# Feed-forward block of an encoder layer: the second norm's sum of squares on POOL, the order of the last weight sum's products, and the buffers of the late halves' weights

## The chip, the cores and the metric

The kernel runs on one core of one Trainium2 chip. The metric is the device time of one execution in microseconds (us), the median of several runs. The core's engines are PE (TensorE, matmuls), DVE (VectorE), ACT (ScalarE), POOL (GpSimd) and SP (SyncE, which here only issues DMAs). Each works through its own list of instructions strictly in order and waits, where an operand or a buffer isn't ready, with everything behind it in the list waiting too.

## The reference

The kernel computes one layer of an encoder trunk on 1024 tokens of width 1024: two groups of mixing heads, an output projection, a squared-ReLU MLP with hidden width 4096, and a gated embedding. What matters here is the MLP, whose input is normalised:

```python
z = jnp.einsum('bsd,df->bsf', rms_norm(h, norm2_g[i]), w_ff1[i])
h = h + jnp.einsum('bsf,fd->bsd', jnp.square(jax.nn.relu(z)), w_ff2[i])
```

The norm divides each token by the root of its mean square, which is a positive factor. The kernel therefore multiplies the un-normalised h with the weights first and applies the factor (the tile `Rb`, one value per token, spread over all partitions) to the products afterwards.

## The kernel before

All matmuls take 32-bit numbers that are split into a rounded part (hi) and the rest (lo), and make three passes: hi with hi, hi with lo, lo with hi. ACT writes a hi part and DVE the lo part (`split`, L138 and L141). A matmul instruction multiplies 128 rows with 512 columns.

The first MLP matmul (FF1) runs in 16 chunks c of 256 hidden columns. Chunks 2 to 15 use a scheme with seven products of 512x512 blocks in place of eight: the blocks of h (tiles `b`, made once) meet four weight tiles per chunk that `sw_prep` makes from the raw weights: a (raw), then after four sums of weight blocks (L231 to L234) b, c and d, where d is the weight sum `s` that only the last product, named s1, reads. Every product is 4 k-steps of 3 passes, so a chunk is 7 x 12 = 84 matmuls. The sums over the products (L260, in chunk 2 L1284) are DVE's. The four weight sums are DVE's in chunks 2 and 3 and POOL's from chunk 4 on. Chunk 2 is `first_prods`, which takes three products one after the other and then interleaves the other four by k-step.

Beside chunk 2, `squares` (L1241 to L1247) sums the squares of h, eight tiles of 1024 tokens in two halves of 512: ACT squares one half tile into `sq`, and an add collects it into `Rb`; the first half's seven adds are POOL's, the second half's DVE's. `sq` has one buffer for each half, so the next square of a half waits for the add of the one before. The sums then go through PE (`n2ps`, L167), DVE (`n2ms`), POOL (`n2rs`, the root), PE again (`n2R`, L179, spreads it) and ACT into `Rb` (L180). From then on `finish(c)` applies it: ReLU times `Rb` on DVE (L1355), the square on ACT (L1356), and `z_blocks` makes block sums on POOL (L1370 to L1376) and stores all of it to four arrays in DRAM, one for each sweep of the second matmul. The stores stand in the queues of SP and ACT.

Chunks 0 and 1 are done without the scheme. Their halves over the first 512 tokens come early (`first_half`), the other halves after chunk 15 (`second_half`, matmuls `p0b` and `p1b`, 48 each), with weights `w1q` that `plain_w` loads and splits into the same ring of two hi and two lo buffers (pool `wp`) in which the chunks' weights and the second matmul's weights live.

The second MLP matmul (FF2, L1503 `f_P`) runs in four sweeps over the chunks, in the order 2, 0, 1, 3. Of sweep 2, `ff2_early` prepares the first three chunks: it loads z back (`zr`), splits it (`zh` on ACT, L1342, and `zl` on DVE) and splits the weights. The order of instructions on each engine comes from a scheduler that works from the program's order, its buffers and its own estimates.

Tiles made with `utile` take a buffer of a ring of 16; the blocks of h, the block sums `tz` and the z tiles live in it too.

Of the kernel before, what the change touches and what calls it, by code (L numbers as in the profile page):

```python
# [14 lines left out]
ALU = mybir.AluOpType  # L15
# [44 lines left out]
def tile_block(ctx, tc, xT, pT, w_in, w_out, w_ff1, w_ff2, w_gate, w_up, vecs, gate_b, rpbp, con,  # L60
# [3 lines left out]
    V, S, G, TE = nc.vector, nc.scalar, nc.gpsimd, nc.tensor  # L64

    def dump(name, ap):
        if name in dbg:
            nc.sync.dma_start(dbg[name], ap)
# [9 lines left out]
    def utile(name):  # L78
        return big.tile([P, T], F32R, tag="u", bufs=16, name=name)

    def utile32(name):
        return big.tile([P, T], F32, tag="u", bufs=16, name=name)
# [24 lines left out]
    Rb = cp.tile([P, T], F32, name="Rb")  # L107
# [27 lines left out]
    def split(pool, raw, n, tag, name, bufs=None, act_hi=True, lo_eng=None, hl=None):  # L135
        hi, lo = hl or [pool.tile([P, n], F32R, tag=tag + x_, name=name + x_, bufs=bufs) for x_ in "hl"]
        if act_hi:
            mark["hi"] = S.activation(hi, raw, AF.Copy).ins  # L138
        else:
            V.tensor_copy(hi, raw)  # L140
        mark["lo"] = (lo_eng or V).tensor_tensor(lo, raw, hi.bitcast(F32), op=ALU.subtract).ins  # L141
        return hi, lo
# [13 lines left out]
    def wview(w, k0, k1, c0, c1):  # L156
        return w[k0 * P : k1 * P, c0:c1].rearrange("(k p) n -> p k n", p=P)

    def passes(ahi, alo, bhi, blo):
        return ((ahi, bhi), (ahi, blo), (alo, bhi))  # L160
# [189 lines left out]
    with tc.tile_pool(name="m0", bufs=2) as m0:  # L350
# [57 lines left out]
        for e in range(8):  # L408
            up = htile(f"up{e}")
            es = slice(e * P, (e + 1) * P)  # L410
            for hf in range(2):
                hs = slice(hf * 512, (hf + 1) * 512)
# [301 lines left out]
    with tc.tile_pool(name="m1", bufs=2) as m1:  # L714
# [159 lines left out]
        def natten_first():  # L874

            kr, qr = raw_load(1, wp, "wr", 3), raw_load(0, wp, "wr", 3)
            yield
            kh, kl = htile("kh0", F32R), htile("kl0", F32R)
            for half in range(2):
                for _ in k_part(0, kr, kh, kl, half):  # L880
                    pass
            yield
            qs = [q_views(htile(f"q0_{rb}", F32R)) for rb in range(2)]
            for rb in range(2):
                for _ in q_part(0, qr, *qs[rb], rb):
                    pass
            nat[0] = [kh, kl, *qs]
            yield

        pre = natten_first()  # L890
# [31 lines left out]
    with tc.tile_pool(name="m2", bufs=2) as m2, tc.tile_pool(name="m2p", bufs=2, space=PSUM) as m2p:  # L922
# [169 lines left out]
        def prep(n):  # L1092

            pr, u = divmod(n, 8)
            if pr and u == 1:
                late.append(q_part(pr, qrs.pop(pr), *nat[pr][3], 1))
            if pr == 3:
                return
            if u in (3, 4):
                late.append(k_part(pr + 1, krs[pr + 1], nat[pr + 1][0], nat[pr + 1][1], u - 3))  # L1100
            if u == 5:
                late.append(q_part(pr + 1, qrs[pr + 1], *nat[pr + 1][2], 0))
# [15 lines left out]
        with tc.manual_schedule():  # L1118
# [9 lines left out]
            for n in range(NU):  # L1128
# [41 lines left out]
                if n in (1, 4, 6):  # L1170
                    j = {1: 0, 4: 1, 6: 2}[n]
# [20 lines left out]
    with tc.tile_pool(name="ff1", bufs=1) as ff1:  # L1192
# [46 lines left out]
        def squares():  # L1239

            sq = utile32("sq2")  # L1241
            for k in range(KT):
                for half in range(2):
                    hs = slice(half * 512, (half + 1) * 512)
                    S.activation((sq if k else Rb)[:, hs], hres[k][:, hs], AF.Square)
                    if k:
                        (V if half else G).tensor_tensor(Rb[:, hs], Rb[:, hs], sq[:, hs], op=ALU.add)  # L1247

        def plain_w(nm, f, hl=None):

            r = wp.tile([P, T], F32, tag="wr", name=f"{nm}_{f}r", bufs=3)
            nc.sync.dma_start(r.rearrange("p (k n) -> p k n", n=P), wview(w_ff1, 0, 8, f * P, (f + 1) * P))
            return [t_.rearrange("p (k n) -> p k n", n=P) for t_ in split(wp, r, T, "w", f"{nm}_{f}", hl=hl)]
# [14 lines left out]
        def first_prods(nm, w, z):  # L1268

            c11, c12, c21, u2 = z[0][:, 0:512], z[0][:, 512:], z[1][:, 0:512], z[1][:, 512:]  # L1270
            names = (("11", "11"), ("12", "21"), ("s4", "22"), ("s2", "t2"), ("s3", "t3"), ("22", "t4"), ("s1", "t1"))
            ps = {an: ps_(f"{nm}_{an}_{bn}") for an, bn in names}

            def part(an, bn, j):
                for i, (x_, y_) in enumerate(passes(w[an][0][:, j], w[an][1][:, j], *B[bn, j])):
                    TE.matmul(ps[an], x_, y_, start=j == 0 and i == 0, stop=j == 3 and i == 2)

            for an, bn in names[:3]:
                for j in range(4):
                    part(an, bn, j)  # L1280
            for j in range(4):
                for an, bn in names[3:]:
                    part(an, bn, j)
            add = lambda o, a, b: V.tensor_tensor(o, a, b, op=ALU.add)  # L1284
            S.activation(u2, ps["11"], AF.Copy)
            add(c11, u2, ps["12"])
            add(u2, u2, ps["s2"])
            add(c12, u2, ps["s4"])
            add(u2, u2, ps["s3"])
            add(c21, u2, ps["22"])  # L1290
            add(c12, c12, ps["s1"])
            add(u2, u2, ps["s1"])

        def prep(c, mid=None):
            s1 = ff1.tile([P, 512], F32, tag="s1", name=f"s1_{c}")
            return sw_prep(f"w1_{c}", [wview(w_ff1, 0, 8, (2 * c + f) * P, (2 * c + f + 1) * P) for f in range(2)],
                           s1, V if c < 4 else G, mid)

        def ff2_early(c):
            return zsplit(utile32(f"zr2_{c}"), utile(f"zh2_{c}"), utile(f"zl2_{c}"), zd[2][:, c]), w2_blocks(2, c)  # L1300
# [39 lines left out]
        def zsplit(raw, hi, lo, src):  # L1340
            nc.sync.dma_start(raw, src)
            S.activation(hi, raw, AF.Copy)  # L1342
            dv.append(V.tensor_tensor(lo, raw, hi.bitcast(F32), op=ALU.subtract).ins)  # L1343
            return hi, lo
# [37 lines left out]
        def relu2(z, hs):  # L1382
            V.scalar_tensor_tensor(z, z, 0.0, Rb[:, hs], op0=ALU.max, op1=ALU.mult)
            S.activation(z, z, AF.Square)
# [40 lines left out]
        for e in range(8):  # L1425
            dump(f"h1_{e}", hres[e])

        def second_half(c):

            zb, z0 = utile32(f"z{c}c"), utile32(f"z{c}d")  # L1430
            nc.sync.dma_start(z0, zd[2][:, c])
            for i, hs in enumerate((h0, h1_)):
                plain(f"p{c}b{i}", [wq.pop(0)], b12, bs("22"), ((4, 5, 6, 7), (0, 1, 2, 3)), (zb[:, hs],))
                if (c, i) != (1, 1) and len(wq) < 2 and wn:
                    wq.append(plain_w("w1q", wn.pop(0)))
                relu2(zb[:, hs], h1_)
            z_blocks(c, zb[:, h0], zb[:, h1_], z0[:, h1_], z0[:, h0])

        for c in range(3, NC_):
            products(c, w, 0)  # L1440
            if c == NC_ - 1:
                b12 = []
                for j in range(4):
                    t_ = ff1.tile([P, T], F32R, tag="b", bufs=NB, name=f"b12_{j}")
                    hi, lo = t_[:, h0], t_[:, h1_]
                    S.activation(hi, hres[j][:, h1_], AF.Copy, scale=vcol(V_G2, j))
                    V.scalar_tensor_tensor(lo, hres[j][:, h1_], vcol(V_G2, j), hi.bitcast(F32), op0=ALU.mult, op1=ALU.subtract)
                    b12.append((hi, lo))

            rs2 = []  # L1450
            sw_prods(f"p{c}", w, B, zt[c], 1, ps_, (lambda: rs2.append(sumsq_to_rstd(Rb, range(KT), "n2"))) if c == 3 else None)
            if c == 3:
                bcast_rstd(rs2[0], range(KT), "n2")
                finish(2)
            if c + 1 < NC_:
                w = prep(c + 1)
            else:
                wn = [2, 3]
                wq = [plain_w("w1q", f) for f in range(2)]
            finish(c)  # L1460
            if c in (5, 6):
                z0 = utile32(f"z{c - 5}b")
                nc.sync.dma_start(z0, zd[2][:, c - 5])
                for hs in (h0, h1_):
                    relu2(z0[:, hs], h0)
                nc.sync.dma_start(zd[2][:, c - 5], z0)
        pre = [ff2_early(0)]
        second_half(0)
        second_half(1)
        pre += [ff2_early(1), ff2_early(2)]  # L1470


    with tc.tile_pool(name="ff2", bufs=2) as ff2:
# [56 lines left out]
        half = lambda r, t, j: hres[4 * r + j][:, t * 512 : (t + 1) * 512]  # L1530
# [53 lines left out]
        op, _ = ff2_sweep(2, 0, ("P2", "P1"), pre, {}, 0)  # L1584
        op, _ = ff2_sweep(0, 1, ("P3", "P6"), op, {}, 2)
# [10 lines left out]
        op, _ = ff2_sweep(1, 3, ("P5", "P7"), op, {EC + ES * c: [(early, c)] for c in range(NE)}, 1)  # L1596
# [103 lines left out]
```

## Time and profile before

| | us |
|---|---|
| runs | 1416.90, 1417.74, 1419.88; median 1417.74 |
| profiled execution, its own time | 1419.03 |
| its span, first to last instruction | 1417.3 |
| PE busy | 1334.9 (94%) |
| DVE busy | 902.3 (64%) |
| ACT busy | 599.0 (42%) |
| POOL busy | 517.6 (37%) |

The span is the stretch that the trace covers; the 1.7 us between it and the execution's own time lie around it. The granted clock, a mean over the span, is 0.965 of full speed. A busy share is a mean over stages with different limits, so it says only which engine to look at first; where an engine stood still is read from the waits, and when, from the timeline.

### The profile page before, as it was taken

Reading aid. Unit: us, or ns where it says so; the run is one execution under the profiler, and the core shown is the slowest. Engines: PE = TensorE matmul, PEld = TensorE weight load, DVE = VectorE, ACT = ScalarE, POOL = GpSimd, SP = SyncE. Lnnn points to the kernel's source line nnn. Section 1 sums busy time; section 2 is a strip of 40 time slices with the busy share of each in tenths; the row PEclk is TensorE's granted clock in tenths of the full one; section 3 lists DMA queues with packets and bytes.
Section 4 is the critical chain, followed back from the end, with each engine's and each line's share of the span. In section 5 each row is a group of like instructions: output and inputs, shape, how many; then the busy total and the mean of one; then the engine's idle time right before and its main releaser. Section 6 shows DMA issues by size and latency. Waiting matters only on the chain. (4 is left out here: it accounts for less than half of the span.)

```text
span 1417.3 us, 19403 instructions
## 1 busy us (share of the span) xinstructions
PE 1334.9 (94%) x7139; PEld 1110.6 (78%) x7139; DVE 902.3 (64%) x1422; ACT 599.0 (42%) x985; POOL 517.6 (37%) x406
## 2 busy tenths in 40 slices
PE   7999999999999889999899999999699899999998
PEld 6988778799888567787777788887488678888887
DVE  4486886665762646578556766675247898559443
ACT  7353443364554535535333333343234234445321
POOL 2215675463421111100256665654102661007422
PEclk9999999999998899999999999999899899999999
DMA  8543333475323644213234555447866683452342
GB/s 282 199 148 93 107 108 105 173 225 160 109 68 124 186 141 133 93 60 105 60 104 156 178 164 163 153 143 239 292 202 205 202 263 105 151 161 73 101 146 82
DMA packets 158158, 211.27 MB, mean 149 GB/s; under 512 B 17904, under 2 KB 106992, under 8 KB 158064
## 3 DMA queue, kind: packets, MB, share of 16 engines
q1 hardware_dynamic: 149968, 192.07, 42.7%
q10 hardware_dynamic: 6624, 12.06, 2.5%
q0 software_dynamic: 1472, 5.92, 1.2%
q8 instruction: 56, 0.92, 0.3%
q14 instruction: 38, 0.31, 0.1%
HBM read 155.79 MB, written 54.21 MB: 148 GB/s over the span
## 5 line engine op out<-in xcount | busy, mean ns | idle before, releaser
L1343 DVE TENSOR_TENSOR zl<-zr,zh 128x1024 fp32r<-128x1024 f32 x56 | 79.8, 1432 | 15.5 <-ACT zh L1342 15.5
L966 POOL TENSOR_SCALAR pc<-pc,st 128x288 f32<-128x288 f32 (+1 forms) x32 | 17.6, 548 | 159.6 <-DVE st L961 128.0
L1324 POOL TENSOR_TENSOR w2re<-sk,w2re 128x512 f32<-128x512 f32 x16 | 32.0, 2002 | 113.6 <-DVE sk L1323 103.2
L1342 ACT ACTIVATE zh<-zr 128x1024 fp32r<-128x1024 f32 x56 | 58.3, 1047 | 17.1 <-DMA zr<-zd 17.1
L956 ACT ACTIVATE pc<-pc,st 128x288 f32<-128x288 f32 (+1 forms) x64 | 36.3, 569 | 57.9 <-DVE st L955 57.9
L1503 PE MATMUL f_P<-zl,w2h 128*128 128x512 f32 x128 | 52.9, 413 | 5.4 <-DVE zl L1343 5.3
L955 DVE CUSTOM_DVE_ANT_1 pc<-sc,tab 128x288 f32<-128x288 f32 (+1 forms) x64 | 29.9, 504 | 41.9 <-DMA tab<-tabU 23.7
L1503 PE MATMUL f_P<-zh,w2h 128*128 128x512 f32 x128 | 51.5, 402 | 1.2 <-ACT zh L1342 1.2
L1503 PE MATMUL f_P<-zh,w2l 128*128 128x512 f32 x128 | 51.7, 404 | 0.0
L1572 PE MATMUL g<-gh,wg_h 128*128 128x512 f32 (+1 forms) x136 | 51.7, 380 | 0.0
L1572 PE MATMUL g<-gl,wg_h 128*128 128x512 f32 (+1 forms) x136 | 51.2, 377 | 0.0
L1572 PE MATMUL g<-gh,wg_l 128*128 128x512 f32 (+1 forms) x136 | 51.1, 377 | 0.0
L1526 POOL TENSOR_TENSOR h<-h,evP 128x512 f32<-128x512 f32 x8 | 14.8, 1887 | 98.3 <-ACT evP L1517 98.3
L790 POOL TENSOR_SCALAR wv<-vh,wj 128x129 f32<-128x129 f32 x56 | 31.0, 556 | 54.1 <-PE num L791 49.6
L1370 POOL TENSOR_TENSOR tz<-z,z 128x512 f32<-128x512 f32 x14 | 18.6, 1330 | 72.3 <-ACT z L1356 72.3
L260 DVE TENSOR_TENSOR z<-z,p_s_t 128x512 f32<-128x512 f32 x52 | 34.5, 683 | 15.9 <-PE p_s_t L256 14.6
L138 ACT ACTIVATE w_bh<-w_0r 128x1024 fp32r<-128x1024 f32 x14 | 14.9, 1062 | 68.3 <-POOL w_0r L234 59.5
L1355 DVE SCALAR_TENSOR_TENSOR z<-z,Rb 128x1024 f32<-128x1024 f32 x28 | 41.3, 1486 | 3.6 <-ACT Rb L180 3.6
L1578 DVE TENSOR_TENSOR z<-g,Rb 128x512 f32<-128x512 f32 (+1 forms) x17 | 11.0, 659 | 43.4 <-PE g L1572 37.5
L997 PE MATMUL pv<-pT,vw 128*64 128x128 f32 (+1 forms) x384 | 31.9, 295 | 6.1 <-DVE pT L986 3.2
L1356 ACT ACTIVATE z<-z 128x1024 f32<-128x1024 f32 x28 | 29.5, 1057 | 19.2 <-DVE z L1355 19.1
L1329 ACT ACTIVATE w2h<-w2ro 128x512 fp32r<-128x512 f32 x16 | 10.1, 632 | 63.9 <-PE f_P L1503 21.1
(861 smaller groups left out, 4780.3 us busy)
## 6 DMA issues: line engine op xcount, KB each, us to landing
zr<-zd SPq DMA_DIRECT2D x56, 512.0 KB
w2r<-w_ff SPq DMA_DIRECT2D x48, 256.0 KB
zd<-z ACTq DMA_DIRECT2D x42, 256.0 KB
zd<-tz SPq DMA_DIRECT2D x32, 256.0 KB
w2re<-w_ff SPq DMA_DIRECT2D x16, 512.0 KB
w2ro<-w_ff SPq DMA_DIRECT2D x16, 512.0 KB
w_0r<-w_ff SPq DMA_DIRECT2D x14, 512.0 KB
w_1r<-w_ff SPq DMA_DIRECT2D x14, 512.0 KB
```

The source lines that it names most:

```text
L260: mark["add"] = V.tensor_tensor(o, a, b, op=ALU.add).ins
L790: G.tensor_scalar(wv, vh[:, c, 0:129], wj[:, col], 1.0, op0=ALU.mult, op1=ALU.mult)
L955: V.tensor_tensor_reduce(pb, sc.rearrange("p a b -> p (a b)"), tab[:, s], -1.0, -NEG, ALU.add, ALU.min, st[:, 0:1])
L956: S.activation(pb, pb, AF.Exp, scale=-1.0, bias=st[:, 0:1], accum_out=st[:, 1:2])
L997: TE.matmul(pv[e0 : e0 + 64, cb], vws[pr][: 4 * kw, cb, rb + j, e0 : e0 + 64], pT[s][: 4 * kw, j], start=j == 0, stop=j == 2)
L1324: G.tensor_tensor(a21, s1, a11, op=ALU.subtract)
L1342: S.activation(hi, raw, AF.Copy)
L1343: dv.append(V.tensor_tensor(lo, raw, hi.bitcast(F32), op=ALU.subtract).ins)
L1355: V.scalar_tensor_tensor(z_, z_, 0.0, Rb, op0=ALU.max, op1=ALU.mult)
L1356: S.activation(z_, z_, AF.Square)
L1503: pe_last = TE.matmul(ps[n, e], a, b, start=st and k == 0, stop=sp and k == 2)
L1572: TE.matmul(ps, x_, y_, start=k == 0 and i == 0, stop=k == KT - 1 and i == 2)
```

## The change

It has five parts. All 14 adds of `squares` go to POOL. In `first_prods` the product s1, which reads the weight sum d, comes behind all others in place of being interleaved with three of them. The four weight sums of chunk 4 go from POOL to DVE. The late halves' weights go to buffers of the 16-buffer ring in place of the two-buffer ring. The preparation of sweep 2's chunk 1 is written ahead of the first late half and that of chunk 2 between the two late halves; both stood behind them.

```diff
 def squares():
-                        (V if half else G).tensor_tensor(Rb[:, hs], Rb[:, hs], sq[:, hs], op=ALU.add)
+                        G.tensor_tensor(Rb[:, hs], Rb[:, hs], sq[:, hs], op=ALU.add)
 def first_prods(nm, w, z):
             for j in range(4):
-                for an, bn in names[3:]:
+                for an, bn in names[3:6]:
                     part(an, bn, j)
+            for j in range(4):
+                part(*names[6], j)
 def prep(c, mid=None):
-                           s1, V if c < 4 else G, mid)
+                           s1, V if c < 5 else G, mid)
+        def late_w(f):
+            return plain_w("w1q", f, (utile(f"w1qh{f}"), utile(f"w1ql{f}")))
 def second_half(c):
-                    wq.append(plain_w("w1q", wn.pop(0)))
+                    wq.append(late_w(wn.pop(0)))
...
-                wq = [plain_w("w1q", f) for f in range(2)]
+                wq = [late_w(f) for f in range(2)]
...
-        pre = [ff2_early(0)]
+        pre = [ff2_early(0), ff2_early(1)]
         second_half(0)
+        pre.append(ff2_early(2))
         second_half(1)
-        pre += [ff2_early(1), ff2_early(2)]
```

**ACT beside chunk 2.** The first difference is on ACT between the end of chunk 2's weights and chunk 3's. `sq` is a square of one half of one tile `h`; `w_2_dh` is the hi part of chunk 2's weight sum d.

```order
-L1245 ACTIVATE sq_7042<-h_4943 128x512
-L1245 ACTIVATE sq_7042<-h_4998 128x512
-L1245 ACTIVATE sq_7042<-h_5137 128x512
-L1245 ACTIVATE sq_7042<-h_5196 128x512
-L1245 ACTIVATE sq_7042<-h_6546 128x512
+L1245 ACTIVATE sq_7042<-h_4943 128x512 x2
+L1245 ACTIVATE sq_7042<-h_4998 128x512 x2
+L1245 ACTIVATE sq_7042<-h_5137 128x512 x2
+L1245 ACTIVATE sq_7042<-h_5196 128x512 x2
+L1245 ACTIVATE sq_7042<-h_6546 128x512 x2
 L138 ACTIVATE w_2_dh<-s_2_6874 128x512
```

With the two of the tile ahead of these, 7 squares stood in front of `w_2_dh` and 12 do now; the second half's squares came beside chunk 4's weights before.

**PE in chunk 3 and at its end.** The spreading of the norm (`n2R`) now stands between the last product of chunk 3 and the first of chunk 4.

```order
 L256 MATMUL p_s_t_7172<-bt_3_6913,w_3_dh 128x512 x2
 L256 MATMUL p_s_t_7172<-bt_3_6913,w_3_dl 128x512
+L179 MATMUL n2R_7187<-cn,n2rs 128x128 x4
+L179 MATMUL n2R_7193<-cn,n2rs 128x128 x4
 L256 MATMUL p_12_21_7272<-b2h_6552,w_4_ah 128x512
```

Before, these two rows stood 20 matmuls into chunk 4. The sums that they need (`n2ps`) stand within chunk 3 now, 28 and 60 of its matmuls in; before, half of them stood in chunk 4.

**SP behind chunk 15.** `zr_0`, `zr_1` and `zr_2` are the z of sweep 2's first chunks, read back; `tz_8963`, `z_0_8832` and `z_1_8833` are chunk 15's block sums; `tz_9057` and `tz_9126` are those of the two late halves. Before, in two pieces of the list:

```order
L1252 DMA w1q_3r<-w_ff 128x8x128
L1341 DMA zr_0_8973<-zd_108 128x1024
L1363 DMA zd_106<-tz_8963 128x512
L1363 DMA zd_107<-tz_8963 128x512
...
L1341 DMA zr_4_9283<-zd_108 128x1024
L1310 DMA w2r_4_9289<-w_ff 128x512
L1363 DMA zd_107<-tz_9126 128x512
L1363 DMA zd_106<-tz_9126 128x512
L1363 DMA zd_107<-z1c 128x512
L1363 DMA zd_109<-z1d 128x512
L1341 DMA zr_1_9136<-zd_108 128x1024
```

And in the change, in one piece:

```order
L1312 DMA w2r_1_8992<-w_ff 128x512 x2
L1252 DMA w1q_2r<-w_ff 128x8x128
L1252 DMA w1q_3r<-w_ff 128x8x128
L1312 DMA w2r_2_9086<-w_ff 128x512
L1343 DMA zr_0_8973<-zd_108 128x1024
L1365 DMA zd_106<-tz_8963 128x512
L1365 DMA zd_107<-tz_8963 128x512
L1365 DMA zd_107<-z_0_8832 128x512
L1365 DMA zd_109<-z_1_8833 128x512
L1343 DMA zr_1_8986<-zd_108 128x1024
```

`zr_1` went from behind the second late half's stores to behind chunk 15's; `zr_0` now has a load of chunk 2's weights (`w2r_2`) ahead of it.

## Rows read from the trace of the kernel before

**Rows 1.** Waits of PE over the whole span: line, releaser, us in total, times, longest.

```profile
PE f_P L1503 <- ACT zh L1342: 15.2, 2, 14.1
PE p_s_t L1276 <- ACT w_dh L138: 3.4, 1, 3.4
```

**Rows 2.** Windows: length; busy us of PE, PEld, DVE, ACT, POOL; clock; DMA share; GB/s.

```profile
694.30:715.25 20.95, 20.14 (x93) 16.74 (x92) 14.29 (x19) 6.72 (x9) 3.30 (x2) 1.00 0.17 50
715.25:743.54 28.29, 24.82 (x102) 19.36 (x100) 13.52 (x14) 10.47 (x13) 14.62 (x10) 0.88 0.39 130
743.54:767.30 23.76, 21.41 (x86) 16.89 (x85) 17.04 (x19) 6.42 (x7) 16.02 (x12) 0.93 0.48 166
828.86:847.90 19.04, 19.04 (x86) 15.77 (x85) 12.27 (x14) 6.37 (x7) 11.51 (x8) 1.00 0.48 153
962.98:1014.18 51.20, 36.04 (x146) 27.78 (x144) 23.12 (x19) 18.00 (x22) 20.89 (x12) 0.87 0.79 265
```

**Rows 3.** Timeline of PE, end of chunk 2 (start, us, instruction, idle before).

```profile
689.06 0.73 PE L1276 MATMUL p_s_t<-bt,w_dh 128*128 128x512 f32 x2 [3.35 <-ACT w_dh L138]
...
691.04 1.05 PE L1276 MATMUL p_s_t<-bt,w_dh 128*128 128x512 f32 x2
691.89 0.63 PE L1276 MATMUL p_s_t<-bt,w_dl 128*128 128x512 f32 x1
...
695.21 0.95 PE L167 MATMUL n2ps<-ones,Rb 128*128 128x1 f32 x8
```

**Rows 4.** Timeline of ACT, beside chunk 2.

```profile
679.75 0.63 ACT L1245 ACTIVATE sq<-h 128x512 f32<-128x512 f32 x1 [1.23 <-POOL Rb L1247]
...
688.39 0.61 ACT L138 ACTIVATE w_dh<-s 128x512 fp32r<-128x512 f32 x1
```

**Rows 5.** The adds of line L1247 by engine: min/median/max ns, first and last start.

```profile
L1247 POOL TENSOR_TENSOR Rb<-Rb,sq x7: 1260/1290/1637, 678.1 to 690.6; 128x512 f32<-128x512 f32 x7
L1247 DVE TENSOR_TENSOR Rb<-Rb,sq x7: 683/690/1004, 708.5 to 721.5; 128x512 f32<-128x512 f32 x7
```

**Rows 6.** Timeline of PE in chunk 4.

```profile
723.09 1.32 PE L167 MATMUL n2ps<-ones,Rb 128*128 128x1 f32 x8
...
726.40 1.17 PE L179 MATMUL n2R<-cn,n2rs 128*128 128x128 f32 x8 [1.42 <-POOL n2rs L171]
```

**Rows 7.** Timeline of ACT, chunk 4.

```profile
727.09 1.12 ACT L180 ACTIVATE Rb<-n2R 128x512 f32<-128x512 f32 x2 [6.24 <-PE n2R L179]
...
741.94 0.60 ACT L267 ACTIVATE z<-p 128x512 f32<-128x512 f32 x1 [4.13 <-DMA zd<-z]
```

**Rows 8.** Timeline of PE, first chunks of sweep 2.

```profile
973.86 0.84 PE L1503 MATMUL f_P<-zh,w_0h 128*128 128x512 f32 x3
...
1006.44 1.22 PE L1503 MATMUL f_P<-zh,w_1h 128*128 128x512 f32 x2 [14.10 <-ACT zh L1342]
```

**Rows 9.** Timeline of SP: `zr_0` and `zr_1`.

```profile
966.11 0.52 SPq L1341 DMA_DIRECT2D zr<-zd  x1
...
1000.74 0.42 SPq L1341 DMA_DIRECT2D zr<-zd  x1
```

**Rows 10.** Timeline of ACT: `zh_0` and `zh_1`.

```profile
971.17 1.06 ACT L1342 ACTIVATE zh<-zr 128x1024 fp32r<-128x1024 f32 x1 [0.93 <-DMA zr<-zd]
...
1005.33 1.06 ACT L1342 ACTIVATE zh<-zr 128x1024 fp32r<-128x1024 f32 x1 [7.40 <-DMA zr<-zd]
```

**Rows 11.** Timeline of DVE behind chunk 15.

```profile
964.38 1.22 DVE L141 TENSOR_TENSOR w1q_1l<-w1q_1r,w1q_1h 128x1024 fp32r<-128x1024 f32 x1
965.52 2.35 DVE L1355 SCALAR_TENSOR_TENSOR z<-z,Rb 128x1024 f32<-128x1024 f32 x2
```

**Rows 12.** Timeline of POOL: last sum of chunks 14 and 15, and one in sweep 0.

```profile
956.84 1.28 POOL L1376 TENSOR_TENSOR z<-z,tz 128x512 f32<-128x512 f32 x1
...
975.15 2.28 POOL L1376 TENSOR_TENSOR z<-z,tz 128x512 f32<-128x512 f32 x1
...
1113.45 6.98 POOL L1324 TENSOR_TENSOR w2re<-sk,w2re 128x512 f32<-128x512 f32 x1 [4.23 <-issue]
```

## The prediction

> **What bounds the kernel now.** I read the page's shares first: PE is busy 94% of the span, no other engine over 64%. The time is PE's, so what a change can give back is the time in which PE stands still or runs at its lower clock. The waits of PE come next [rows 1]: the longest single one in the span is 14.1 us, for a `zh` at the start of sweep 2, and 3.4 us go to the wait for the weight sum d of chunk 2. Then windows, one for each chunk [rows 2]: a chunk at full speed takes 19.04 us (84 matmuls, 0.227 each). Chunk 4, with 28.29 us, loses 9.25 and chunk 5, with 23.76, loses 4.7, part of it because the clock fell (0.88 and 0.93 over the window). The stretch from the first late half to chunk 2 of sweep 2 takes 51.20 us for 144 matmuls, 32.6 at full speed: 18.6 lost. The change works on these two places, which I call A (chunks 2 to 5) and B (chunk 15 to sweep 2).
>
> **Why A loses.** The norm's chain is late. The second half's adds start on DVE at 708.5 and end at 722.2 [rows 5]; the last sums through PE follow at 723.09, the spreading at 726.40 after a wait for POOL [rows 6], `Rb` at 727.09 [rows 7]. Everything of `finish(2)` and `finish(3)` then falls into chunk 4 at once, and ACT waits 4.13 us for stores to drain before it may copy out chunk 4's first product at 741.94 [rows 7]. PE meets this as late weights for chunks 4 and 5.
>
> **Place A, the sum.** All times are on the scale of the trace before.
>
> 1. The adds. With both halves on POOL the squares alternate between two halves of `sq`, so the add's wait for its square (the squares waited 1.23 us for the add and not the reverse [rows 4]) goes and adds run back to back. The first took 1.64, the others 1.26 to 1.30 [rows 5]; I take 1.31 from start to start. Add 14 ends at 678.1 + 1.64 + 13 x 1.31 = 696.8, against 722.2 on DVE.
> 2. The price. ACT's 12 squares now stand ahead of `w_2_dh`, and the twelfth waits for add 10, which ends at 678.1 + 1.64 + 9 x 1.31 = 691.5. With the square (0.63) and `w_2_dh` (0.61) [rows 4] that is 692.8, where it was 689.0. PE had waited 3.35 us for it [rows 3]. Three matmuls of the product before it move ahead of the wait, so 12 remain in place of 15; at the half clock each takes (691.89 - 691.04) / 2 = 0.425 [rows 3]. Nine so and three at 0.227 make 4.5 us: chunk 3 starts at 697.3, before at 694.30 [rows 2]. **+3.0.**
> 3. Chunk 3 now holds both halves of the sums (0.95 [rows 3] and 1.32) and the spreading (1.17 [rows 6]): 19.04 + 3.44 = 22.5, before 20.95. **+1.5**, chunk 4 at 719.8. The sums are ready (697) before PE asks for them (28 matmuls in, 703.7).
> 4. Chunk 4 is free of the chain: 19.04 in place of 28.29, **-9.25**. The weight sums of chunk 4 on DVE are four instructions of some 0.69 in place of four of some 1.65 on POOL, off the path: DVE is 14.3 of 20.95 us busy in chunk 3 [rows 2], and without seven adds of 0.69 it has 4.8 us more.
> 5. Chunk 5: stores and block sums of chunk 2 come some 7 us sooner, and the 4.13 us wait of ACT should go. I leave 0.5 of the 4.7 lost. **-4.2.** Chunk 6 then starts 9.0 earlier. Chunks 6 to 8 keep their small losses, as their order is the same.
>
> Bounds: step 2 from 0 (PE finds the sum ready) to +6.3 (every add 1.64); step 4 from -9.25 to -4 (weights late again); step 5 from -4.7 to 0. A lies between -12.5 and +3.8, and I take **-9.0**.
>
> One rule speaks against the first part. POOL takes a median of 1290 ns for the same add for which DVE takes 690 [rows 5]. The Trainium skill, GPSIMD Engine Reference, "4.1 Engine selection", says to give elementwise work with two inputs to VectorE, as GpSimd is about twice as slow. The trace agrees on the ratio, 1.87; by that rule the change puts seven adds of 690 ns at 1290 ns each, a loss of 4.2 us, if the adds were the bound where they stood. But they were not started before 708.5, since ACT's queue held the second half's squares behind chunk 3's weights; the start counts 30 us and the speed 4.
>
> **Place B, the sum.** `zr_1` is issued at 1000.74, behind the stores of the last late half, and `zh_1` follows 4.6 us later [rows 9, 10]. PE runs dry, waits 14.10 and restarts at 1006.44 at the lower clock [rows 8]. In the change `zr_1` stands behind chunk 15's stores. But new things stand ahead of it:
>
> 1. `w1q`'s first hi part takes the buffer of chunk 14's `tz` and stands ahead of `w_15_dh` on ACT. It waits for POOL's last sum of chunk 14, which ends at 958.1 [rows 12]; with 1.06, 0.63 and a lo part of some 1.3 chunk 15's last product has what it needs at 961.1, some 0.7 late. **0.7 lost.**
> 2. `zr_0` now waits in SP's queue for the buffer that `w2r_2` fills, which is free when DVE has split chunk 1's weights. That stands behind ReLU times `Rb` of chunk 15. The pair took 2.35 from 965.52, with one lo part (1.22) ahead of it [rows 11]; one more lo part comes ahead and one behind: 965.5 + 0.7 + 1.2 + 2.4 + 1.2 = 971.0, where it was 966.11 [rows 9]. From issue to `zh_0` took 5.1 to its start and 1.06 more [rows 9, 10], so PE has it at 977.1. The 48 matmuls end at 963.7 + 10.9 = 974.6: **2.5 lost**. Then 9 matmuls, to 979.1.
> 3. Chunk 15's sums on POOL ended at 977.4 [rows 12]; with the square some 1.2 us later 978.6, `zr_1` then at 979.0, and `zh_1` after 4.6 and 1.06 at 984.7. **5.6 lost**, and 2 for the lower clock after it (the last time the restart cost about as much).
> 4. 87 matmuls are left, 19.7.
>
> From the late half's usual start: 0.7 + 10.9 + 2.5 + 2.0 + 5.6 + 2 + 19.7 = 43.4, before 51.2: **-7.8**. Bounds: -18.6 if both waits vanish, 0 if the wait only moves.
>
> **Sum.** -9.0 and -7.8 make -16.8: the profiled execution would take 1402.2, and against the median, 1.3 below it, **1401 us**. What lies behind chunk 2 of sweep 2 I leave at its length: the change writes nothing there, and it follows PE.
>
> **Rivals.**
>
> *Both places give all.* If `zr_0` and `zr_1` come in time, B is -18.6, and with A -9.0 the time is 1417.74 - 27.6 = 1390. For it: 4.6 us from issue to use is short against 51. Against it: the queue rows of step 2. Chance 0.15.
>
> *Only one place gives.* The weight sums on DVE or the squares delay chunk 3's weights and A comes to 0, or the wait for `zh_1` moves to another buffer and B does: 1408.7 to 1410, in a mixed case up to 1413. For it: ACT and SP are strictly in order, and each has a new wait ahead of old work. Chance 0.19.
>
> *The change does nothing.* What comes early waits again where sweep 0 begins, where POOL and DVE are late anyway: 1415 to 1420. Against it: what waits there is made on the way, not at a fixed time. Chance 0.06.
>
> *POOL's adds drag (slower).* One POOL sum of the same size took 6.98 us where DVE was busy nearly throughout [rows 12], while the median add took 1.29 [rows 5]. If the 14 adds take t each, chunk 3 starts 10 x (t - 1.31) later. At t = 3.0 that eats 16.9, the whole gain; at 3.4 the time is 1417.74 - 16.8 + 20.9 = 1422. For it: DVE has more to do beside them. Against it: the seven adds in the trace never took over 1.64. The Trainium skill, GPSIMD Engine Reference, "1. Specifications", lists POOL's interfaces to SBUF as shared with VectorE and names contention with DVE instructions of two SBUF inputs, which these are; the trace has both the steady row and the dragged one. Chance 0.06.
>
> **How the numbers follow.** A measurement of this kernel can tell some 0.2%, 2.8 us, from no change. My forecast (1395 to 1406) has 0.54, the first rival 0.15, the second 0.19, the third 0.06, the fourth 0.06. The range 1390 to 1413 leaves out half of the first rival and the last two. Faster has 0.54 + 0.15 + 0.18 = 0.87, the same 0.06, slower 0.07.
>
> **What would show it.** In the profile after: 14 adds of line L1247 on POOL, 1.3 us apart; a wait of PE for `w_2_dh` of about 6.4 us in place of 3.4; chunk 4 in 19 to 20 us and chunk 6 starting at about 758; no wait of 14 us for `zh`, but two of about 2.5 and 5.6 near 975 and 980 on the old scale; sweep 2's chunk 2 some 17 us earlier than 1014.18. I am wrong if adds take over 2 us, if chunk 4 still takes over 24 us, or if a wait of over 10 us for a `zh` remains.

## The result, and the profile after

The changed kernel takes **1400.7 us** (median of 4 runs, 1400.03 to 1407.04) against 1418.68 for the kernel before beside it; the ratio is 0.9883, 95% interval 0.9856 to 0.9910. In a second set it was 1405.05 against 1417.27, ratio 0.9909 (0.9893 to 0.9924). The forecast was 1401 with a range of 1390 to 1413.

The profiled execution has a span of 1405.3 us against 1417.3. It was the slowest of the four (1407.04), so the stages read from it below lie some 6 us above the median in their sum. The waits of PE over the whole span, line, releaser, total, times, longest:

```profile
PE p_s_t L1276 <- ACT w_dh L138: 5.7, 1, 5.7
PE f_P L1508 <- ACT zh L1344: 5.2, 3, 2.1
...
PE p_s_t L1276 <- DVE w_dl L141: 3.0, 1, 3.0
```

The 14.1 us of [rows 1] are gone; the longest wait for a `zh` is 2.1 (line 1503 is 1508 now). The wait for the hi part of chunk 2's weight sum d grew from 3.4 to 5.7, and a wait for its lo part, 3.0 us, is new.

The windows by stage that answer to [rows 2], in the same columns: chunks 2, 3, 4 and 5, then the late halves up to chunk 2 of sweep 2, then everything from chunk 2 to the late halves.

```profile
673.21:704.12 30.91, 22.14 (x85) 17.32 (x84) 17.18 (x18) 15.36 (x24) 17.70 (x14) 0.80 0.16 51
704.12:726.50 22.38, 22.38 (x110) 18.82 (x108) 13.55 (x19) 4.40 (x6) 1.65 (x1) 0.97 0.17 48
726.50:746.02 19.52, 19.44 (x87) 15.86 (x86) 15.35 (x16) 9.55 (x11) 14.14 (x9) 1.00 0.66 228
746.02:767.65 21.63, 19.93 (x85) 15.55 (x84) 12.64 (x14) 6.32 (x7) 15.04 (x11) 1.00 0.45 146
962.10:1002.66 40.56, 36.46 (x145) 29.10 (x144) 17.34 (x18) 15.66 (x19) 14.22 (x11) 0.92 0.75 242
673.21:962.10 288.89, 276.16 (x1202) 224.83 (x1200) 189.54 (x204) 105.58 (x127) 164.18 (x111) 0.98 0.45 145
```

Chunk 4 fell from 28.29 to 19.52 and its clock is 1.00. Chunk 2 grew: it starts at 669.90 before and 673.21 after, and takes 30.91 where it took 694.30 - 669.90 = 24.40. Below, **A** is the stretch from chunk 2's first matmul to the first matmul of the late halves, and **B** from there to chunk 2 of sweep 2. Before, A is 962.98 - 669.90 = 293.08 and B 51.20; after, 288.89 and 40.56. So B gave 10.6 us and A, in this execution, 4.2. What lies ahead took 3.3 more.

Each run of the next section has its own profile, and the same four stretches can be read from each; again is the changed kernel once more, best is two of the edits together. The table has them in us: what lies ahead of chunk 2, A, B, and the rest of the span.

| run | ahead | A | B | rest |
|---|---|---|---|---|
| before | 669.9 | 293.1 | 51.2 | 403.1 |
| after | 673.2 | 288.9 | 40.6 | 402.6 |
| again | 673.7 | 285.9 | 40.6 | 403.0 |
| a_only | 670.5 | 285.3 | 51.3 | 403.4 |
| b_only | 672.9 | 293.6 | 40.7 | 403.1 |
| no1 | 667.3 | 291.6 | 38.8 | 402.6 |
| no2 | 672.3 | 284.3 | 39.3 | 402.9 |
| no3 | 673.3 | 290.5 | 40.3 | 403.1 |
| no5 | 670.0 | 284.8 | 51.5 | 403.0 |
| s2_first | 669.2 | 285.3 | 39.1 | 403.2 |
| s2_lo | 672.6 | 287.7 | 42.6 | 402.6 |
| mixed | 671.2 | 278.0 | 40.1 | 402.7 |
| zr_ahead | 670.0 | 284.8 | 40.1 | 403.0 |
| best | 673.0 | 278.0 | 41.3 | 403.2 |

Two things follow at once. The rest is 402.6 to 403.4 everywhere: what is won before sweep 2's chunk 2 is not given back. And what lies ahead of chunk 2 spreads over 6.4 us although no edit touches it; this alone puts several us between single executions, so the stages decide more sharply than the totals.

### The profile page after: what moved, and what is told of

It reads as the page before. It is cut to its first block, busy times and chain, and to the rows that moved or that the text cites. A ratio compares the mean times of both kernels' runs of the same rounds, so it can differ in the third digit from the quotient of the medians.

```text
span 1405.3 us, 19398 instructions
## 1 busy us (share of the span) xinstructions
PE 1330.1 (95%) x7139; PEld 1109.6 (79%) x7139; DVE 903.2 (64%) x1419; ACT 598.5 (43%) x985; POOL 513.6 (37%) x409
## 4 chain that ended last, share of the span: by engine, by line
PE 56%; DVE 5%; DMA 5%; POOL 3%; issue 3%; ACT 2%; SPq 0%; DVEq 0%; POOLq 0%; ACTq 0%
PE f_P L1508 18%; PE op L1025 6%; PE p_s_t L256 6%; PE g L1577 6%; PE p L256 4%; PE p_s L256 2%; PE p_t L256 2%; DMA nr<-qnd 2%; PE pv L997 1%; PE pt L977 1%; PE o1p L312 1%; DMA tab<-tabI 1%; POOL Rb L1247 1%; PE p1a L1263 1%; PE sc L947 1%
## 5 line engine op out<-in xcount | busy, mean ns | idle before, releaser
L1326 POOL TENSOR_TENSOR w2re<-sk,w2re 128x512 f32<-128x512 f32 x16 | 27.0, 1686 | 99.9 <-DVE sk L1325 85.2
L955 DVE CUSTOM_DVE_ANT_1 pc<-sc,tab 128x288 f32<-128x288 f32 (+1 forms) x64 | 29.9, 504 | 40.6 <-DMA tab<-tabU 22.0
L1577 PE MATMUL g<-gl,wg_h 128*128 128x512 f32 (+1 forms) x136 | 51.3, 377 | 0.0
L1577 PE MATMUL g<-gh,wg_l 128*128 128x512 f32 (+1 forms) x136 | 51.2, 377 | 0.0
L1531 POOL TENSOR_TENSOR h<-h,evP 128x512 f32<-128x512 f32 x8 | 14.8, 1886 | 98.3 <-ACT evP L1522 98.3
L1247 POOL TENSOR_TENSOR Rb<-Rb,sq 128x512 f32<-128x512 f32 x14 | 17.7, 1310 | 70.6 <-ACT sq L1245 70.6
L138 ACT ACTIVATE w_bh<-w_0r 128x1024 fp32r<-128x1024 f32 x14 | 14.8, 1061 | 56.3 <-POOL w_0r L234 53.9
L138 ACT ACTIVATE w_ah<-w_0r 128x1024 fp32r<-128x1024 f32 x14 | 14.9, 1062 | 54.8 <-PE p_t L256 46.7
```

The source lines that it names most:

```text
L1247: G.tensor_tensor(Rb[:, hs], Rb[:, hs], sq[:, hs], op=ALU.add)
L1577: TE.matmul(ps, x_, y_, start=k == 0 and i == 0, stop=k == KT - 1 and i == 2)
```

## The experiments

### Each place alone

a_only takes back parts 4 and 5, b_only parts 1 to 3:

```diff
a_only
-            return plain_w("w1q", f, (utile(f"w1qh{f}"), utile(f"w1ql{f}")))
+            return plain_w("w1q", f)
...
-        pre = [ff2_early(0), ff2_early(1)]
+        pre = [ff2_early(0)]
         second_half(0)
-        pre.append(ff2_early(2))
         second_half(1)
+        pre += [ff2_early(1), ff2_early(2)]
b_only
-                        G.tensor_tensor(Rb[:, hs], Rb[:, hs], sq[:, hs], op=ALU.add)
+                        (V if half else G).tensor_tensor(Rb[:, hs], Rb[:, hs], sq[:, hs], op=ALU.add)
...
-                for an, bn in names[3:6]:
+                for an, bn in names[3:]:
                     part(an, bn, j)
-            for j in range(4):
-                part(*names[6], j)
...
-                           s1, V if c < 5 else G, mid)
+                           s1, V if c < 4 else G, mid)
```

a_only:

> Parts 1 to 3 alone (squares on POOL, product s1 last, chunk 4's weight sums on DVE); the late halves' buffers and the order of sweep 2's preparation are as before. If the two places are independent: from the first matmul of chunk 2 to the first of the late halves 288.9 us as with the whole change (293.1 before), from there to chunk 2 of sweep 2 51.2 us as before (40.6 with the whole change), so about 4 us less than before. If place B's gain needs the earlier norm, place B shows less than 51.2 here.

b_only:

> Parts 4 and 5 alone (buffers of the late halves' weights, order of sweep 2's preparation); squares, s1 and chunk 4's sums as before. If the places are independent: 293.1 us from chunk 2 to the late halves as before, 40.6 us from there to chunk 2 of sweep 2, about 11 us less than before. The rival, that place B only gains because place A runs ahead, gives 46 us or more there.

a_only is 1412.1 against 1417.45, ratio 0.9958 (0.9943 to 0.9973); b_only is 1405.55, ratio 0.9928 (0.9907 to 0.9949). In a_only B is 51.3, in b_only A is 293.6 and B 40.7: the places are independent. What didn't fit is A in a_only: 285.3 in place of the 288.9 that nearly the same instructions took in the profile after.

### Who gets in: POOL's adds and DVE's lo part

Of the 3.6 us between the two, 0.6 lie in chunk 15 (19.64 against 19.04). The greater part, 2.5, lies in chunk 2, and there in one DVE instruction, the lo part of d. DVE's timeline in the changed kernel, then POOL's:

```profile
689.09 0.69 DVE L1286 TENSOR_TENSOR z<-z,p_s 128x512 f32<-128x512 f32 x1
695.40 4.23 DVE L141 TENSOR_TENSOR w_dl<-s,w_dh 128x512 fp32r<-128x512 f32 x1 [5.62 <-ACT w_dh L138]
```

```profile
681.38 17.70 POOL L1247 TENSOR_TENSOR Rb<-Rb,sq 128x512 f32<-128x512 f32 x14 [70.63 <-ACT sq L1245]
```

The 14 adds end at 681.38 + 17.70 = 699.08, and the lo part, which takes 0.69 in chunk 3 with POOL idle, ends at 699.63, 0.55 later: it stood until POOL's last add was done. The sum at 689.09, one of whose inputs lies in PSUM, took its usual 0.69 in the midst of the adds, as did the one before it. So in this stretch the instruction with two inputs in SBUF is kept out, and only that. Two runs test it, the change without part 1 (as in the diff of b_only), and the change unedited once more.

no1:

> The whole change without part 1: the second half's seven adds are DVE's again, so POOL has 0.74 us pauses between its adds. Theory (POOL's adds back to back keep DVE's two-input instruction out): the lo part of chunk 2's weight sum d takes 0.7 to 1.4 us in place of 4.2, and PE's wait for it (3.0) is gone; but the norm comes late, chunk 4 takes 27 us or more again, so the whole is 3 to 8 us slower than the change. Rival (the lo part is slow for another reason, its hi part or its place on DVE): it takes about 4 us here too.

again:

> The changed kernel once more, nothing edited. In its first profile the lo part of chunk 2's weight sum took 4.23 us on DVE and ended with POOL's last add; with the same instructions but for sweep 2's preparation it took 1.79 in the run with parts 1 to 3 alone. Theory (at each border between two adds, DVE and POOL compete for the port, and who wins is chance): 1.2 to 1.8 us or 3 to 4.5 us here, nothing between, and the stretch from chunk 2 to the late halves is 285 us in the first case and 289 in the second. Rival (parts 4 and 5 change it): 4.2 us again.

DVE's and POOL's timelines in no1, then in again:

```profile
686.45 1.35 DVE L141 TENSOR_TENSOR w_dl<-s,w_dh 128x512 fp32r<-128x512 f32 x1 [3.29 <-ACT w_dh L138]
```

```profile
685.98 1.27 POOL L1247 TENSOR_TENSOR Rb<-Rb,sq 128x512 f32<-128x512 f32 x1 [0.74 <-ACT sq L1245]
```

```profile
695.92 1.80 DVE L141 TENSOR_TENSOR w_dl<-s,w_dh 128x512 fp32r<-128x512 f32 x1 [5.62 <-ACT w_dh L138]
```

```profile
681.91 19.18 POOL L1247 TENSOR_TENSOR Rb<-Rb,sq 128x512 f32<-128x512 f32 x14 [70.66 <-ACT sq L1245]
```

In no1 POOL pauses 0.74 us between adds; the lo part starts within an add that ends at 687.25 and ends 0.55 after it. In again the adds are back to back, DVE gets in at the next border, POOL's series takes 19.18 in place of 17.70 (its last two adds 1.74 and 2.26 with DVE's instructions between them), and A is 285.9. So the same program had 4.23 in one execution and 1.80 in the other, so parts 4 and 5 need not be the cause; a_only, no2, no3, no5 and zr_ahead had about 1.8 as well. The pause is then not needed for DVE to get in. That DVE's instruction waits for the end of a POOL add is shown: in all of these profiles it ended 0.55 us after one. That it is chance who wins a border is what two executions of one program suggest; what decides it stays open.

no1 is 1405.58 against 1417.45, ratio 0.9921 (0.9906 to 0.9937). Its A is 291.6, 5.7 us more than in again: the late norm is back, with 25.43 us for chunk 4, a little less than the 27 that I expected. So part 1 is worth some 6 us of A, where DVE gets in at the first border. The medians alone would not show it: the ratio of again is 0.9909 (0.9893 to 0.9924).

### Parts 2 and 3

no2 takes back part 2, no3 part 3, each with the lines that the diff of b_only shows.

no2:

> The whole change without part 2: product s1 is interleaved again with three others. The hi part of the weight sum d still stands behind 12 squares, and PE meets it three matmuls earlier: its wait grows by 0.7 us and fifteen matmuls in place of twelve follow at the lower clock, about 1 us; slower than the change by 0.5 to 3 us. The lo part is as slow (about 4 us) by the theory of POOL's adds, and blocks PE from the third matmul on in both orders.

no3:

> The whole change without part 3: the four weight sums of chunk 4 are POOL's again, behind its 14 adds, and the root of the norm stands behind two of them. By step 4 of the sum they are off the path on either engine: two sums of 1.3 to 1.7 us between the adds' end (some 26 us after chunk 2's start) and the norm's sums, which come at 45; chunk 3 and 4 as in the change within 1 us, no difference that the median can show. Rival (POOL is the bound there): chunk 4 takes 21 us or more in place of 19.5.

no2 is 1402.7, ratio 0.9891 (0.9873 to 0.9909), with A 284.3 against 284.8 to 285.9 in again, a_only, no5 and zr_ahead, which have it and in which the lo part took 1.8 too. I expected it 0.5 to 3 us slower; **part 2 gives nothing that these stages can show**. PE's wait for the hi part is 6.2 in place of 5.7, but the interleaved order has other matmuls to fill the wait for the lo part, 0.6 in again, and no2 has none.

no3 is 1407.95 against 1417.57, ratio 0.9936 (0.9924 to 0.9948), and A is 290.5: **part 3 is worth some 5 us**, and I had put it at nothing. Chunk 5 takes 26.37 in place of 21.6. PE, ACT and DVE in its timelines:

```profile
748.18 0.80 PE L256 MATMUL p<-b,w_al 128*128 128x512 f32 x1 [4.34 <-DVE w_al L141]
```

```profile
725.57 1.06 ACT L138 ACTIVATE w_bh<-w_0r 128x1024 fp32r<-128x1024 f32 x1 [4.07 <-POOL w_0r L234]
726.53 1.06 ACT L180 ACTIVATE Rb<-n2R 128x512 f32<-128x512 f32 x2
...
740.00 0.60 ACT L267 ACTIVATE z<-p 128x512 f32<-128x512 f32 x1 [4.33 <-DMA zd<-z]
```

```profile
743.27 0.69 DVE L260 TENSOR_TENSOR z<-z,p 128x512 f32<-128x512 f32 x1 [6.88 <-DMA zd<-z]
746.90 1.22 DVE L141 TENSOR_TENSOR w_al<-w_0r,w_ah 128x1024 fp32r<-128x1024 f32 x1
```

The weights b of chunk 4 wait 4.07 for POOL's sums, and `Rb` stands behind them on ACT: it begins 2.55 us after chunk 4 (723.98), where in again it begins with it (724.02 and 724.12). Everything of `finish` is later by that, the stores too, and ACT may copy out chunk 4's first product only when a store of z has left the buffer. The sums over chunk 4's products stand behind that copy on DVE and wait for a store of their own, until 743.27, where in again they begin at 739.74; chunk 5's lo part stands behind them. ACT's wait is the 4.13 of [rows 7] again: the earlier adds alone did not remove it. This chain is read from the timelines; that part 3 is worth the 5 us is what no3 shows.

### Part 5: the order on SP

no5 takes back only the order of sweep 2's preparation (the second piece of the diff of a_only).

> The whole change without part 5: the late halves' weights have their own buffers, but sweep 2's chunks 1 and 2 are prepared behind both late halves, as before. The load of z for chunk 1 then stands behind the stores of the second late half on SP again. Theory (the order on SP is what the 14 us wait is made of): the wait for zh of 13 to 15 us is back, place B takes 50 to 52 us in place of 40.6, and the kernel is about 11 us slower than the change. Rival (the two-buffer ring held the weights back, and the order does little): place B stays below 45 us.

It is 1410.7 against 1417.57, ratio 0.9953 (0.9941 to 0.9965), and B is 51.5. PE's timeline:

```profile
997.49 1.22 PE L1508 MATMUL f_P<-zh,w_1h 128*128 128x512 f32 x2 [11.53 <-ACT zh L1344]
```

The long wait is back with the order, if a little shorter than the 13 to 15 us that I expected, although the weights have their own buffers. All of B's gain comes with part 5; part 4 alone gives none. Part 5 without part 4 was not tried.

### What is left in B

PE and SP in the changed kernel, place B:

```profile
975.18 1.64 PE L1508 MATMUL f_P<-zh,w_0h 128*128 128x512 f32 x3 [2.03 <-ACT zh L1344]
...
981.17 0.96 PE L1508 MATMUL f_P<-zh,w_1h 128*128 128x512 f32 x3 [2.06 <-ACT zh L1344]
```

```profile
968.92 0.38 SPq L1343 DMA_DIRECT2D zr<-zd  x1
...
974.66 0.40 SPq L1343 DMA_DIRECT2D zr<-zd  x1
```

The two waits are there that the prediction put at 2.5 and 5.6. zr_ahead tries to remove the first, by keeping chunk 2's weights behind the load of z (`mark` remembers an instruction, and what stands under `after` is issued only behind it):

```diff
-            nc.sync.dma_start(raw, src)
+            mark["zr"] = nc.sync.dma_start(raw, src).ins
...
-        pre = [ff2_early(0), ff2_early(1)]
+        pre = [ff2_early(0)]
+        mark["z0"] = mark["zr"]
+        pre.append(ff2_early(1))
         second_half(0)
-        pre.append(ff2_early(2))
+        with after("z0"):
+            pre.append(ff2_early(2))
```

> The change, with the load of chunk 2's weights kept behind the load of z for chunk 0 on SP. By step 2 of place B the load of z was held by that one row: it should now issue about 5 us sooner, zh of chunk 0 is there before the 48 matmuls end, PE's first wait (2.0 to 2.5 us) goes, and part of the lower clock behind it. The second wait (1.3 to 2.9) stays, as chunk 1's z stands behind chunk 15's stores; PE reaches it earlier, so it may grow by up to 2. Place B 38 to 39.5 us in place of 39.1 to 40.6; the whole 1 to 2.5 us faster than the change, or nothing if the second wait takes it all.

```profile
973.65 1.65 PE L1511 MATMUL f_P<-zh,w_1h 128*128 128x512 f32 x3 [5.74 <-ACT zh L1344]
```

The first wait is gone and the second has grown to 5.74; B is 40.1, the median 1401.78 against 1417.57, ratio 0.9901 (0.9880 to 0.9921), no different from the change. (B lies between 38.8 and 42.6 in all runs that keep parts 4 and 5, so a gain of 1 to 2 us could not be seen in a single profile.) The end of B's last wait hangs on the load of chunk 1's z: 973.65 is 18.8 us after the late halves' first matmul (954.83), and in the change it was 981.17 - 962.10 = 19.1, whether PE came early or late.

### What is left in A

PE's longest wait is for the hi part of d, which stands behind 12 squares on ACT, and ACT behind POOL. s2_first takes the product s2 ahead of two others, which frees the buffer for the hi part sooner; s2_lo also moves the lo part to POOL:

```diff
s2_first
             for j in range(4):
-                for an, bn in names[3:6]:
+                part(*names[3], j)
+            for j in range(4):
+                for an, bn in names[4:6]:
                     part(an, bn, j)
s2_lo, with the above
-            hi, lo = split(wp, t_, n, "w", f"{nm}_{x_}")
+            hi, lo = split(wp, t_, n, "w", f"{nm}_{x_}", lo_eng=G if (nm, x_) == ("w1_2", "d") else None)
```

s2_first:

> The change, with product s2 of chunk 2 taken ahead of s3 and 22 in place of interleaved with them. It frees the buffer that the weight sum's hi part waits for 24 matmuls (5.4 us) sooner, and the hi part moves ahead of seven of the twelve squares. PE's wait for the hi part should go (5.7 us before). The lo part on DVE now falls into the middle of POOL's adds: if DVE wins a border early, 1 to 3 us and PE doesn't wait; if it stands until POOL's last add, 10 us or more and PE waits as long as before. Chunk 3's first weights stand behind 13 squares, so chunk 3 starts at the earliest 25 us after chunk 2 in place of 28.5 to 31: 3 to 5 us faster than the change, or nothing if the lo part stands.

s2_lo:

> As s2_first, but the lo part of the weight sum is computed on POOL, between its adds 5 and 6, so that it doesn't compete for the port. It should take 1.3 us on POOL, always. PE doesn't wait for d at all; what is left is the wait for chunk 3's first weights behind 13 squares: chunk 3 starts 25 to 26 us after chunk 2, 282 us from chunk 2 to the late halves, 3 us faster than the change. The rival to the queue theory, that PE's wait came from the buffer and not from ACT's squares, expects chunk 3 at 20 us and 277.

The waits for d are gone in both, and A gained nothing: it is 285.3 and 287.7, against 285.9 in again. The medians are 1400.76 (ratio 0.9882, 0.9864 to 0.9900) and 1403.98 (0.9904, 0.9882 to 0.9926), beside 1405.05 (0.9909) for again; the interval of the first overlaps that of again. PE's timeline of s2_first, then DVE's:

```profile
694.50 1.22 PE L256 MATMUL p<-b,w_ah 128*128 128x512 f32 x2 [6.06 <-ACT w_ah L138]
```

```profile
682.76 1.85 DVE L141 TENSOR_TENSOR w_dl<-s,w_dh 128x512 fp32r<-128x512 f32 x1 [1.03 <-ACT w_dh L138]
684.65 1.67 DVE L231 TENSOR_TENSOR s<-w_1r 128x512 f32<-128x512 f32 x1
686.36 1.68 DVE L232 TENSOR_TENSOR w_1r<-w_0r,w_1r 128x512 f32<-128x512 f32 x1
```

The wait has moved to chunk 3's first weights, which stand behind 13 squares, and the restart at the lower clock went with it (the first pair of matmuls takes 1.22 where a pair at full speed takes 0.62): chunk 2 is 25.3 and chunk 3 24.7 long. In s2_first chunk 2 gave 3.2 us against again and chunk 3 took 2.8 of them back. The error in both expectations was to leave out that restart. Three DVE instructions in a row took 1.67 to 1.85, one border each. This suggests that the queue has to be cleared as a whole. mixed adds to s2_lo that later squares stand behind chunk 3's weights:

```diff
 sw_prep, put
+            mark[nm + x_] = mark["hi"]
 squares
-                    S.activation((sq if k else Rb)[:, hs], hres[k][:, hs], AF.Square)
+                    with after(*{3: ('w1_3a',), 4: ('w1_3a',), 5: ('w1_3b',), 6: ('w1_3b',), 7: ('w1_3c',)}.get(k, ())):
+                        S.activation((sq if k else Rb)[:, hs], hres[k][:, hs], AF.Square)
```

> As s2_lo, and the squares are spread: four stand ahead of chunk 2's d, four behind the hi part of chunk 3's a, four behind that of b, two behind that of c. By the queue theory no weight then stands behind more than four squares: chunk 2 takes 19 to 21 us, chunk 3 20 to 24, chunk 4 19 to 22 as in the change; from chunk 2 to the late halves 276 to 280 us, 5 to 9 us faster than the change. It is worse than the change if the sums come so late that chunk 4 takes over 25 us again.

It is **1393.77 against 1417.27, ratio 0.9836** (0.9813 to 0.9860), where the change beside it has 0.9909. The windows of chunks 2 and 3 and of A:

```profile
671.23:690.27 19.04, 19.04 (x86) 15.77 (x84) 14.12 (x20) 10.32 (x16) 7.74 (x6) 1.00 0.27 83
690.27:713.51 23.24, 22.23 (x109) 18.14 (x108) 16.21 (x18) 9.12 (x14) 16.82 (x11) 1.00 0.16 46
671.23:949.23 278.00, 272.94 (x1202) 222.41 (x1200) 191.20 (x204) 105.32 (x127) 168.45 (x112) 1.00 0.47 150
```

Chunk 2 of again, in the same columns:

```profile
673.74:702.21 28.47, 22.13 (x86) 17.30 (x84) 15.73 (x18) 15.36 (x24) 19.18 (x14) 0.83 0.18 56
```

In mixed chunk 2 runs its 84 matmuls without a stop, and the clock over all of A is 1.00, where again has 0.83 in chunk 2. The spread squares came on top of the two earlier edits; alone they were not tried. best has mixed and zr_ahead together:

> The edits of mixed and of zr_ahead together. If they are independent: 278 us from chunk 2 to the late halves and 38 to 39.5 from there to chunk 2 of sweep 2, 1 to 2 us less than mixed, 9 to 12 less than the change.

It is 1396.49 against 1417.57, ratio 0.9833 (0.9811 to 0.9855), A 278.0, B 41.3: as mixed, within the noise, so zr_ahead adds nothing that shows. mixed is the simpler of the two and beats both kernels.

## Why the prediction was right, point by point

The total and the direction were right; the two terms were off in opposite directions. A was put at -9.0 and measured -4.2 in the profile after and -7.2 in that of again (293.1 less 285.9); B was put at -7.8 and measured -10.6 twice. The two profiles differ by 4.2 + 10.6 = 14.8 and 7.2 + 10.6 = 17.8 from before in these stages; the forecast was 16.8. The profiled execution itself was put at 1402.2 and took 1407.04. So the hit on the median to within 1 us has luck in it, from two errors that nearly cancel and from the spread of single executions; the median of again, 1405.05, is 4 us above the forecast. One of the signs failed with A: chunk 6 was to start 9.0 us earlier, and in the profile after it starts 94.4 us behind chunk 2's start where it was 97.4, so 3.0 earlier.

- **Step 1 of A, the adds: right in size.** The adds took a median of 1284 ns and the series 17.70 us, where I had 18.7. The rival that POOL's adds drag fell: none took over 1.63 in this profile, and in again only the last took over 2 (2.26). What dragged was the other side, DVE, which none of my cases had.
- **Step 2, the price: the mechanism right, one wait missing.** PE's wait for the hi part is 5.73 (put at about 6.4). But behind it came the wait for the lo part, 3.04 us in the profile after and 0.61 in again, and chunk 2 grew by 6.5 (30.91 less 24.40) and by 4.1, where I had 3.0. The sum has no term for the lo part, although in the kernel before it already took 1.35 us in this place and not 0.69.
- **Steps 3 and 4 of the sum: right.** Chunk 3 took 22.38 (put at 22.5), chunk 4 19.52 (put at 19.04). But step 4 costed part 3 at nothing; no3 shows that it carries some 5 us, and its timelines point to `Rb` behind the weights b on ACT's queue. I had counted DVE's and POOL's time and not what is queued behind the waiting instruction on ACT.
- **Step 5: half of it.** Chunk 5 fell by 2.1, not 4.2. ACT's wait for the store in front of chunk 4's first product went from 4.13 to 1.86, not to nothing, and chunk 5 keeps waits of 0.53 to 0.61 for its weights. Chunk 6 gave 1.5 that I had not counted.
- **B, step 1:** put at 0.7, measured 962.10 - 942.46 = 19.64 for chunk 15, 0.6 over the full speed. **Step 2:** put at 2.5, measured 2.03. **Step 3 is the step that failed:** put at 5.6, measured 2.06. I had taken chunk 15's block sums on POOL as long as before, where the last three took 2.16 to 2.28 (the last in [rows 12]). They took 1.26 to 1.29 now. In the kernel before, POOL's third sum and DVE's split of z beside it:

```profile
972.92 2.27 POOL L1374 TENSOR_TENSOR z<-z 128x512 f32<-128x512 f32 x1
```

```profile
972.26 1.78 DVE L1343 TENSOR_TENSOR zl<-zr,zh 128x1024 fp32r<-128x1024 f32 x1 [0.46 <-ACT zh L1342]
```

And POOL's third and fourth sum in the change:

```profile
971.49 1.29 POOL L1376 TENSOR_TENSOR z<-z 128x512 f32<-128x512 f32 x1
972.96 1.26 POOL L1378 TENSOR_TENSOR z<-z,tz 128x512 f32<-128x512 f32 x1 [0.19 <-PE p0b L1263]
```

Before, DVE split chunk 0's weights and z at that time; in the change its next such instruction begins only at 975.16, so POOL's sums had none of them beside them and `zr_1` could issue at 974.66, 12.6 us after the late halves' first matmul in place of the 15.3 that I had. In zr_ahead DVE's split of z comes early again and falls on one of the sums:

```profile
964.48 2.27 POOL L1376 TENSOR_TENSOR z<-z 128x512 f32<-128x512 f32 x1
```

```profile
964.02 1.58 DVE L1345 TENSOR_TENSOR zl<-zr,zh 128x1024 fp32r<-128x1024 f32 x1 [2.79 <-ACT zh L1344]
```

There the sum takes 2.27 as before, and the load of chunk 1's z is issued 13.6 us after the late halves' first matmul. So the two engines seem to hold each other up here too, this time to the change's good; no run was made for this alone. Against that, the matmuls behind the first wait ran at the lower clock, which I had counted only behind the second.

The rule that I weighed, that POOL is the slower engine for such adds (the Trainium skill, GPSIMD Engine Reference, "4.1 Engine selection"), holds for the single instruction, 1284 ns in this profile against 690 [rows 5]. no1 follows it for seven of the adds, and its A is 5.7 us longer than that of again, though the medians don't tell the two apart. In A, where the instruction starts counted for more. The line on interfaces shared with VectorE (the Trainium skill, GPSIMD Engine Reference, "1. Specifications") was the rival's ground; the traces agree that the two engines hold each other up, but it was PE's wait for DVE's lo part that cost time, up to 3.04 us, and not POOL's series, which grew by 1.5 in again.

## What to carry to other kernels

Before moving work to an idle engine, ask what stands behind it in the queue of the engine that feeds it: the 14 adds took 17.7 us on a POOL that had nothing else to do and were done in time for the norm, but twelve squares on ACT, paced by them, held back the weights that PE waited for, and taking the weights out from behind them (mixed, with two smaller edits) was worth another 8 us of A. A wait that is removed at one place can come back at the next instruction that depends on the same queue (s2_first, zr_ahead), and what it then costs includes the restart at the lower clock. And when the time between two loads matters, order the list of the engine that issues them: here that order, with the buffers that go with it, was worth about 11 us.

## What was not expected of the hardware

While POOL ran these adds, with all operands in SBUF, a 128x512 DVE instruction with two inputs in SBUF that came beside one did not finish before it: it ended 0.55 us after the end of a POOL add. With the adds back to back that was the first border in seven profiles (1.8 us; again, a_only, no2, no3, no5, zr_ahead and s2_first) and the end of the whole series (4.23 us in place of 0.69) in one. DVE instructions with an input in PSUM kept their 0.69 us. With pauses of 0.74 us between POOL's adds DVE got in at the first border in all three profiles (before, b_only and no1, 1.35 us). In the other direction a POOL sum took 6.98 us in sweep 0 [rows 12]. In the same trace DVE ran instructions without a gap from 1108.02 to 1119.27, and the sum ended 1.2 us after the last of them; that DVE held it up is likely by this, but was not tested.
